# An S5 layer with a SwiGLU feed-forward: the last quarter's two sets of lag products move from behind the scan to ahead of its end

## The chip, the cores and the metric

One core of a Trainium2 chip runs the whole program. Its engines each follow their own queue of instructions: PE (matrix products), DVE, ACT and POOL (elementwise work), and SP, which here only issues transfers. The metric is the device time of one execution in microseconds (us); the time before is the median of three executions.

## The reference, cut to what matters

One layer of a diffusion backbone on 1024 latent tokens and 256 context tokens of width 1024, in fp32. With a depth of one, the only mixer is the bidirectional S5 one, followed by a SwiGLU feed-forward and a final norm; only the latent tokens are returned.

```python
def s5_direction(u_ctx, u_lat, lam_re, lam_im, log_step, b_re, b_im, c_re, c_im):
    lam_bar = jnp.exp(lam * jnp.exp(log_step)[:, None])
    b_bar = ((lam_bar - 1.0) / lam)[..., None] * lax.complex(b_re, b_im)
    def run(u, h0):
        bu = jnp.einsum('lgh,gnh->lgn', u, b_bar)
        bu = bu.at[0].add(lam_bar * h0)
        _, h = lax.associative_scan(_linear_combine, (a, bu), axis=0)
        return jnp.einsum('lgn,ghn->lgh', h, c_mat).real, h[-1]
    y_c, h_c = run(u_ctx, 0)      # the context's last state starts the latent scan
    y_l, _ = run(u_lat, h_c)
    return y_c, y_l

# both directions are added, then
y = y + d_skip * h
g = gelu(y)
mixed = g * sigmoid(g @ w_glu + b_glu)
# residual with adaLN gate, RMSNorm, (silu(h @ w1) * (h @ w3)) @ w2, residual, final RMSNorm
```

There are 64 groups of 16 channels, each with 64 complex states in each direction.

## The kernel before, in words

**The mixer.** Eight tokens form a chunk, so there are 32 context and 128 latent chunks. For every chunk and group PE makes one state input, DVE runs the recurrence over chunk ends (`scan`, L839), and the output of a chunk is the sum of two things: what its own eight tokens give each other, a product of the chunk's input with a Toeplitz matrix of 15 lags, and what the state at the chunk's start gives. The 64 groups are worked on as four quarters of 16 groups (q = 0 to 3), or as eight blocks of 8 groups (k = 0 to 7, two to a quarter).

**What sets the order.** Each engine runs its instructions in the order in which the program writes them. For this stage that order is spelled out by two strings of steps, `PROG1` and `PROG2` (L32, L33), which `run` (L954) reads from left to right. DVE's scan is written before `PROG1`; the other engines run through `PROG1` while DVE scans. Between the two strings the PSUM pools of the first stage are closed and a pool of eight banks (`pe8`, tiles named `pe`) is opened in their place. A letter is a kind of step, the number its quarter, block or half:

- C: one of four products that make a quarter's output matrices, two multiplications and an addition on POOL, or the addition elsewhere. C30 to C33 are those of the last quarter.
- K: a set of lag products (`k_mats`, L802), two sets to a quarter, so K6 and K7 are the last quarter's. A set is 72 small matrix instructions on PE into two PSUM banks, which take turns; the banks must hold zeros where no product lands. Then ACT copies each bank (L821) and issues a transfer of each copy to DRAM (L822).
- T: a transfer on SP that reads the lags back as Toeplitz matrices (`toeplitz`, L830). T12 to T15 are the last quarter's.
- P, Y: for blocks 0 to 5, the chunk's own part and the state part of the first half of the latent chunks on PE, and the copies out of PSUM on ACT.
- R, Z, z: copies of the backward direction's states in turned order, on ACT or DVE. Z and z need the end of the scan.
- N, D, H: for blocks 0 to 5, the state part of the second half on PE, its addition on DVE, and the GELU on ACT. Q: both parts of blocks 6 and 7 on PE, after T12 to T15.
- I, J: the transposed output for the gated linear unit, on PE, ACT and DVE. w, l, W: its weights' loads on SP and their split in two fp32r parts on DVE and POOL. g: its first products on PE. b, x, V: the bias, the gate and the split of further weights.
- M, m, F: modulation columns and a row, and the last states between scan steps, on POOL.

Blocks K0 to K5 lie in `PROG1`: one bank is always `kt`, zeroed once, the other one a zeroed `pw` bank for quarters 0 and 1, and `pm` for quarter 2. K6 and K7 are in `PROG2`, each with two banks of the new pool; the steps k6 and k7 take the banks, and DVE sets them to zero (L966) ahead of its own work there.

Of the kernel before, what the change touches and what calls it, by code (L numbers as in the profile page):

```python
# [25 lines left out]
HC = 16  # L26
# [2 lines left out]
MAGIC = 12582912.0  # L29
HOWS = "PPPP PPEE PEEE EEEE"  # L30
ZEN = "VVSVSVSV"
PROG1 = ("A22 B0 A26 C02 G1 A30 A34 C03 A40 K0 A44 A48 C10 K1 L2 A54 G2 C11 A60 F10 C12 F11 C13 T0 T1 T2 T3 A64 M0 M1 K2 R0 P0 Y0 Y1 K3 L3 R1 C20 P1 Y2 Y3 T4 T5 G3 T6 T7 C21 C22 C23 K4 R2 P2 Y4 Y5 K5 R3 P3 Y6 Y7 T8 T9 T10 T11 C30 C31 R4 P4 Y8 Y9 C32 C33 R5 P5 Y10 Y11 M2 m0 F30 F31")  # L32
PROG2 = ("k6 Z0 N0 Z1 Z2 D0 Z3 N1 k7 D1 Z4 H0 H1 K6 N2 D2 H2 K7 T12 T13 T14 T15 N3 Z5 D3 H3 N4 D4 z6 z7 I0 J0 I1 J1 w0 w1 l1 H4 N5 D5 I2 J2 H5 I3 J3 W0 W1 x0 x1 x2 x3"  # L33
         " Q6 H6 I4 J4 Q7 b0 I5 J5 H7 g03 g13 I6 J6 g23 g05 g15 I7 J7 V1 w20 w21 g26 x10 x11 x12 x13")
LOG2E = 1.4426950408889634
LN2H = 0.693359375
# [6 lines left out]
def s5_ffn_kernel(tc, a, out):  # L43
    nc = tc.nc
    V, S, E, PE, SY = nc.vector, nc.scalar, nc.gpsimd, nc.tensor, nc.sync
    ctx = ExitStack()
    with ctx:
        ctx.enter_context(tc.manual_schedule())
        sb = ctx.enter_context(tc.tile_pool(name="sb", bufs=1))
        def region(tag, kb, dt=F32):  # L50
            return sb.tile([P, int(kb * 256)], dt, tag=tag, name=tag)
# [12 lines left out]
        R0 = region("r0", 7)  # L64
# [79 lines left out]
        def pw(shape=(4, P)):  # L144
            return pW.tile([P] + list(shape), F32, tag="w", name="pw", bufs=NW[0])
# [613 lines left out]
        pm = pW.tile([P, 512], F32, tag="m", name="pm")  # L759
# [10 lines left out]
        def zeros(t):  # L770
            S.copy(t, cpk[:, 0:1].to_broadcast([P, 15 * HC]))
            return t

        kt = zeros(pA.tile([P, 15 * HC], F32, tag="r3", name="kt"))
# [24 lines left out]
        def bb(q, d, ri, a_):  # L799
            return BBn[q // 2][:, ri, d, 8 * (q % 2) + a_]  # L800

        def k_mats(q, hq, kts):  # L802

            tiles = [(g_, 2 * gi + hq, kts[g_][32 * gi:32 * gi + HC], slice(64 * g_, 64 * g_ + 64), (64 * g_, 32 * gi))
                     for gi in range(4) for g_ in range(2)]
            for d, c0, c1, ts_ in ((1, 128, 240, slice(7, 0, -1)), (0, 0, 112, slice(6, None, -1))):
                for ri in range(2):
                    for g_, a_, kv, ps, tp in tiles:
                        PE.matmul(kv[:, c0:c1], bb(q, d, ri, a_)[ps], CL[q][ps, ri, d, a_, ts_], start=ri == 0, stop=ri == 1,
                                  tile_position=tp)  # L810
            for g_, a_, kv, ps, tp in tiles:
                l0 = 64 * g_ + HC * (tp[1] // 32)
                PE.matmul(kv[:, 112:128], ident[ps, l0:l0 + HC], KD[ps, q, hq], start=True, stop=False, tile_position=tp)
            for d in range(2):
                for ri in range(2):
                    for g_, a_, kv, ps, tp in tiles:
                        PE.matmul(kv[:, 112:128], bb(q, d, ri, a_)[ps], Cs[q % 2][ps, 0, ri, d, a_], start=False,
                                  stop=d + ri == 2, tile_position=tp)
            for g_ in range(2):
                gq, kx = 2 * hq + g_, KX[2 * hq + g_]  # L820
                S.copy(kx, kts[g_])  # L821
                S.dma_start(KD_[q][:, gq], kx)  # L822
# [131 lines left out]
        def run(prog):  # L954


            for w in prog.split():
                op, i = w[0], int(w[1:])
                if op == "A":
                    ada(i)  # L960
                elif op == "M":
                    mod_cols(i)
                elif op == "k":
                    KT[i] = [pe8([15 * HC]) for _ in range(2)]
                    for kv in KT[i]:
                        V.memset(kv, 0.0)  # L966
                elif op == "K":
                    k_mats(*divmod(i, 2), KT.get(i) or [kt, zeros(pw([15 * HC])) if i < 4 else pm[:, 0:15 * HC]])
                elif op == "L":
                    cs_load(i, S)  # L970
                elif op == "G":
                    cs_sign(i)
                elif op == "B":
                    bb_put(1, bb_turn(1))
                    bb_put(0, bb_turn(0))
                elif op == "C":
                    q, part = divmod(i, 10)
                    for f in cl_ops(q, part, cts[q][part], HOW[q][part]):
                        f()
                elif op == "F":  # L980
                    fill(*divmod(i, 10), *((RW, 0) if i >= 30 else (RC[3], 12)))
                elif op == "T":
                    toeplitz(i)
                elif op == "R":
                    turned(i, 0, HSe[i], S)
                elif op == "Z":
                    turned(i, 1, HSl[i], ENG[ZEN[i]])
                elif op == "z":
                    turned(i, 2, HSq[i], ENG[ZEN[i]])
                elif op == "P":  # L990
                    inner[i] = x_mm(i, pw)
                    states_mm(i, inner[i], 0, HSe[i], False)
                elif op == "Q":
                    inner[i] = x_mm(i, pe8)
                    states_all(i, inner[i], HSq[i])
                elif op == "Y":
                    S.copy(yview(i // 2, i % 2), inner[i // 2][i % 2])
                elif op == "N":
                    late[i] = [pe8([4, T, HC]) for _ in range(2)]
                    states_mm(i, late[i], 1, HSl[i], True)  # L1000
                elif op == "D":
                    for gp, po in enumerate(late[i]):
                        tt(yview(i, gp), po, yview(i, gp), ADD)
                elif op == "H":
                    if i in late:
                        S.activation(Y[:, i], Y[:, i], AF.Gelu_apprx_tanh)
                    else:
                        for gp in range(2):
                            S.activation(yview(i, gp), inner[i][gp], AF.Gelu_apprx_tanh)
                elif op == "I":  # L1010
                    if GH[0] is None:
                        GH[0] = tuple(view(region(t, 16, R32), 0, [4, 8, P]) for t in ("c1", "c0"))
                    late[i] = gt_hi(i, 0)
                elif op == "J":
                    gt_lo(i, 0, late[i])
                elif op == "W":
                    if not WR:
                        W0.append(region("c2", 16, R32))
                        WR.append((view(W0[0], 0, [8 * 256]), view(W0[0], 8, [8 * 256])))
                    v = slice(1024 * i, 1024 * i + 1024)  # L1020
                    split(wr0[i], (WR[0][0][:, v], WR[0][1][:, v]), E, V)
                elif op == "w":
                    cq, h = divmod(i, 10)
                    SY.dma_start(wr0[h], a["w_glu"][cq][:, 1024 * h:1024 * h + 1024])
                elif op == "b":
                    SY.dma_start(bglu, a["b_glu"].to_broadcast([P, D]))
                elif op == "l":
                    load_glu(i)
                elif op == "m":
                    mod_row(0)  # L1030
                elif op == "x":
                    gate(i % 10, slice(4 * (i // 10), 4 * (i // 10) + 4))
                elif op == "V":
                    GR.append(region("ra", 80.5, R32))
                    GH[1] = (view(GR[0], 0, [4, 8, P]), view(GR[0], 16, [4, 8, P]))
                    WR.extend((view(GR[0], kb, [8 * 256]), view(GR[0], kb + 8, [8 * 256])) for kb in (32, 48, 64))
                    split(wraw, WR[i], E)
                elif op == "g":
                    glu_mm(0, i // 10, range(i % 10 + 1))

        KT = {}
        late, W0, WR, PZ, GH, GR = {}, [], [], {}, [None, None], []
        wr0 = [view(RXa, 4, [1024]), view(RW, 0, [1024])]
        bglu = view(RU, 32, [D])
# [5 lines left out]
        def pe8(shape, tag="e", bufs=8):  # L1050
            return pE.tile([P] + list(shape), F32, tag=tag, name="pe", bufs=bufs)
# [51 lines left out]

        HOW = [[{"P": PE, "Y": SY, "E": E, "V": V}[c] for c in h] for h in HOWS.split()]
        run(PROG1)
        psW.__exit__(None, None, None)
        psA.__exit__(None, None, None)
        psE = tc.tile_pool(name="psE", bufs=1, space=bass.MemoryType.PSUM, reuse_waits="tile")
        pE = psE.__enter__()
        run(PROG2)  # L1110
        W0, GR = W0[0], GR[0]
# [93 lines left out]
        for cq in range(4):  # L1205
            for s in range(4):
                k = 4 * cq + s
# [61 lines left out]
        G2 = region("c3", 16, R32)  # L1269
# [420 lines left out]
        for i, (kind, ft, j) in enumerate(seq):  # L1690
# [12 lines left out]
            if kind == "U":  # L1703
# [4 lines left out]
                if (ft, j) in LAST:  # L1708
                    k, h = LAST[ft, j]
# [63 lines left out]
```

## Time and profile before

| | |
|---|---|
| median of 3 executions | 1024.48 us (1022.91 to 1024.67) |
| the profiled execution's own time | 1024.33 us |
| its span, first to last instruction | 1022.5 us |
| PE busy | 962.6 us (94%) |
| DVE, ACT, POOL busy | 785.6, 438.5, 762.7 us |
| mean granted clock of PE | 0.987 of full speed |

A row of the timeline gives the start of a run of like instructions, how long it lasts, the engine, the line of the kernel, the operation, the tile written and the tiles read, and in brackets how long the engine was idle before it and what ended that wait. PEld is the weight load that belongs to a matmul and overlaps with the one before. "Granted clock" is the share of full speed that the chip let PE run at. For fp32 the trace holds two records for each matrix instruction of the program.

### The profile page before, as it was taken

The numbers are of one execution on the slowest core, as the hardware profiler recorded it, in microseconds if no ns is written. First come the engines' busy times: TensorE is split into PE (matmuls) and PEld (weight loads), VectorE is DVE, ScalarE is ACT, GpSimd is POOL, SyncE is SP. The second block draws the span as 40 slices with busy tenths as digits, with TensorE's granted clock in tenths as the row PEclk, the third lists the DMA queues.
The fourth block names the chain that finished last, engine by engine and source line by source line (L and its number), as shares of the span: only waits on it lengthen the run. The fifth ranks groups of instructions, "written<-read, shape, count | busy, mean of one in ns | idle before, by whom it ended". The sixth has DMA issues, their size and how long they took to land. (4 is left out here: it accounts for less than half of the span.)

```text
span 1022.5 us, 18552 instructions
## 1 busy us (share of the span) xinstructions
PE 962.6 (94%) x6988; PEld 774.2 (76%) x6988; DVE 785.6 (77%) x1642; ACT 438.5 (43%) x858; POOL 762.7 (75%) x590
## 2 busy tenths in 40 slices
PE   5987798868999999999999999999999999999996
PEld 1466523658999988778888888888888888888885
DVE  7989799994365778788968768585958778686977
ACT  5477622324353663533334343424333343324337
POOL 5799999991591457879686877778686877777664
PEclk9999999998999999999999999999999999999998
DMA  9765997222622021011212011121212111121205
GB/s 318 292 132 96 276 350 243 91 73 57 235 80 86 2 104 62 21 42 42 83 41 73 32 52 61 43 73 52 73 42 81 41 40 56 45 70 52 72 21 165
DMA packets 48546, 98.96 MB, mean 97 GB/s; under 512 B 4284, under 2 KB 18876, under 8 KB 47176
## 3 DMA queue, kind: packets, MB, share of 16 engines
q1 hardware_dynamic: 43272, 86.64, 25.3%
q0 software_dynamic: 2016, 7.34, 3.8%
q10 hardware_dynamic: 3168, 3.79, 1.1%
q8 instruction: 55, 0.90, 0.4%
q14 instruction: 35, 0.29, 0.1%
HBM read 84.25 MB, written 6.17 MB: 88 GB/s over the span
## 5 line engine op out<-in xcount | busy, mean ns | idle before, releaser
L77 POOL TENSOR_TENSOR c<-rxc,c 128x512 fp32r<-128x512 f32 x128 | 166.6, 1316 | 53.5 <-ACT c L1227 52.7
L1287 PE MATMUL ut<-ra,c 128*128 128x512 f32 x400 | 155.7, 389 | 1.2 <-DVE ra L77 1.2
L1286 PE MATMUL ut<-ra,c 128*128 128x512 f32 x400 | 155.7, 389 | 0.2 <-ACT ra L1227 0.2
L1288 PE MATMUL ut<-ra,c 128*128 128x512 f32 x400 | 155.6, 389 | 0.0
L1227 ACT CAST c<-rxc 128x512 fp32r<-128x512 f32 x128 | 79.1, 622 | 146.8 <-PE xt L1581 53.3
L1581 PE MATMUL xt<-c,c 128*128 128x512 f32 x540 | 129.7, 389 | 0.0
L1581 PEld LDWEIGHTS xt<-c,c 128*128 128x128 f32 x540 | 101.4, 188 | 21.0
L77 DVE TENSOR_TENSOR ru<-ru,xt 128x1024 f32<-128x1024 f32 x90 | 106.8, 1213 | 8.6 <-PE xt L1581 6.6
L77 DVE TENSOR_TENSOR ru<-ut,ru 128x512 f32<-128x512 f32 x98 | 67.1, 686 | 43.1 <-PE ut L1288 37.7
L1287 PEld LDWEIGHTS ut<-ra,c 128*128 128x128 f32 x400 | 75.1, 188 | 17.1 <-POOL rxc L77 1.5
L1286 PEld LDWEIGHTS ut<-ra,c 128*128 128x128 f32 x400 | 75.1, 188 | 16.1 <-ACT ra L1227 0.6
L1288 PEld LDWEIGHTS ut<-ra,c 128*128 128x128 f32 x400 | 75.1, 188 | 15.5
L77 POOL TENSOR_TENSOR c<-rw,c 128x512 fp32r<-128x512 f32 (+1 forms) x29 | 42.5, 1465 | 38.8 <-ACT c L1227 38.2
L1286 PE MATMUL ut<-c,c 128*128 128x512 f32 x160 | 62.3, 389 | 0.8 <-DVE rxa L77 0.8
L77 POOL TENSOR_TENSOR c<-ru,c 128x512 fp32r<-128x512 f32 (+1 forms) x39 | 55.5, 1422 | 10.1 <-ACT c L1227 5.7
L77 POOL TENSOR_TENSOR rxc<-rxc 128x512 f32<-128x512 f32 x40 | 61.5, 1536 | 1.6
L1288 PE MATMUL ut<-c,c 128*128 128x512 f32 x160 | 62.3, 389 | 0.0
L1287 PE MATMUL ut<-c,c 128*128 128x512 f32 x160 | 62.3, 389 | 0.0
L1581 PE MATMUL ut<-c,c 128*128 128x512 f32 x216 | 51.9, 389 | 0.0
L584 PE MATMUL pv<-ru,c 128*64 128x160 f32 x512 | 43.7, 312 | 7.3 <-POOL ru L77 2.6
L77 DVE TENSOR_TENSOR pe<-pe,ru 128x256 f32<-128x256 f32 x64 | 27.4, 428 | 29.5 <-ACT pe L1127 17.4
L77 DVE TENSOR_TENSOR ru<-ru,ut 128x512 f32<-128x512 f32 x76 | 47.2, 678 | 0.7 <-ACT ru L1635 0.5
(449 smaller groups left out, 2576.0 us busy)
## 6 DMA issues: line engine op xcount, KB each, us to landing
c<-in_ada_w SPq DMA_DIRECT2D x46, 256.0 KB
rxc<-in_w SPq DMA_DIRECT2D x38, 256.0 KB
rxc<-in_w SPq DMA_DIRECT2D x19, 512.0 KB
ru<-in_w SPq DMA_DIRECT2D x11, 512.0 KB
rw<-in_w SPq DMA_DIRECT2D x11, 512.0 KB
ra<-in_ada_w SPq DMA_DIRECT2D x10, 512.0 KB
ra<-in_ada_w SPq DMA_DIRECT2D x18, 256.0 KB
ru<-in_xT SPq DMA_DIRECT2D x4, 1024.0 KB
```

The source lines that it names most:

```text
L77: eng.tensor_tensor(out=o, in0=x, in1=y, op=op)
L584: PE.matmul(pv[64 * (i % 2):64 * (i % 2) + 64, ri, c0:c0 + 160], w[:, i, 64 * ri:64 * ri + 64], U[:, 8 * b + 4 * j + i], start=True, stop= ...
L1227: S.copy(o[0], x)
L1286: PE.matmul(pu, wh, bh, start=start, stop=False)
L1287: PE.matmul(pu, wh, bl, start=False, stop=False)
L1288: PE.matmul(pu, wl, bh, start=False, stop=stop)
L1581: PE.matmul(pd, w[:, cs_], b, start=j in (1, 2, 4) and n == 0, stop=n == 2, skip_group_check=j not in (1, 2, 4))
```

## The change

K6 and K7 move out of `PROG2`, to a place in `PROG1` behind Y11 (the copies of block 5) and ahead of M2, m0, F30 and F31. They use the two banks of the third quarter's sets, `kt` and `pm`, for both sets. The steps k6 and k7 and their four memsets go. T12 to T15 stay where they were in `PROG2`.

```diff
-PROG1 = ("A22 B0 ... C32 C33 R5 P5 Y10 Y11 M2 m0 F30 F31")
-PROG2 = ("k6 Z0 N0 Z1 Z2 D0 Z3 N1 k7 D1 Z4 H0 H1 K6 N2 D2 H2 K7 T12 T13 T14 T15 N3 Z5 D3 H3 N4 D4 z6 z7 I0 J0 I1 J1 w0 w1 l1 ...
+PROG1 = ("A22 B0 ... C32 C33 R5 P5 Y10 Y11 K6 K7 M2 m0 F30 F31")
+PROG2 = ("Z0 N0 Z1 Z2 D0 Z3 N1 D1 Z4 H0 H1 N2 D2 H2 T12 T13 T14 T15 N3 Z5 D3 H3 N4 D4 z6 z7 I0 J0 I1 J1 w0 w1 l1 ...
...
-                elif op == "k":
-                    KT[i] = [pe8([15 * HC]) for _ in range(2)]
-                    for kv in KT[i]:
-                        V.memset(kv, 0.0)
                 elif op == "K":
-                    k_mats(*divmod(i, 2), KT.get(i) or [kt, zeros(pw([15 * HC])) if i < 4 else pm[:, 0:15 * HC]])
+                    k_mats(*divmod(i, 2), [kt, zeros(pw([15 * HC])) if i < 4 else pm[:, 0:15 * HC]])
...
-        KT = {}
```

On PE the program before reads as follows from P5 (lines 945 and 922 into `pw`) on. The tiles `pe` are banks of the new pool, lines 809, 813 and 817 are a K set, and line 922 into `pe` is an N step: 64 rows are N0 and N1, then 32 each.

```order
L945 MATMUL pw<-ra,ru 128x128 x8
L922 MATMUL pw<-c_65,ra 64x128 x32
L922 MATMUL pe<-c_63,ra 64x128 x64
L809 MATMUL pe<-c_66,rxa 16x112 x32
L813 MATMUL pe<-r_60 16x16 x8
L817 MATMUL pe<-rxc,rxa 16x16 x32
L922 MATMUL pe<-c_64,ra 64x128 x32
```

K6 stands behind N0 and N1, and N2 follows it; K7 stands in the same way between N2 and N3. In the changed program, at the place where K6 ends and K7 begins, with the waits of each row:

```order
L817 MATMUL kt<-rxc,rxa 16x16
L817 MATMUL pm<-rxc,rxa 16x16
L809 MATMUL kt<-c_66,rxa 16x112 [waits Activation_49]
L809 MATMUL pm<-c_66,rxa 16x112 [waits Activation_49]
L809 MATMUL kt<-c_66,rxa 16x112
```

The two sets now follow each other directly, ahead of N0, and K7's first instruction on each of the two banks waits for ACT, which copies that bank for K6. Behind K7 the N steps stand in a row:

```order
L922 MATMUL pe<-c_63,ra 64x128 [waits DVE_49,Activation_49]
L922 MATMUL pe<-c_63,ra 64x128
L922 MATMUL pe<-c_63,ra 64x128 [waits DVE_49]
L922 MATMUL pe<-c_63,ra 64x128 x31
```

N0's first instruction waits for DVE and for ACT, and its third for DVE's turned copy. On ACT the copies and transfers move as follows (`ru<-pw` ahead of the piece is the copy of P5; line 902 are Z2 and Z4, and the table load belongs to the first GELU):

```order
+L821 COPY r_60<-kt 128x240
+L822 DMA kd_1249<-r_60 128x240
+L821 COPY r_60<-pm 128x240
+L822 DMA kd_1249<-r_60 128x240
+L821 COPY rw<-kt 128x240
+L822 DMA kd_1249<-rw 128x240
+L821 COPY rw<-pm 128x240
+L822 DMA kd_1249<-rw 128x240
 L902 COPY ra<-ra 128x512 x2
-L1006 ACT_TABLE_LOAD
```

Before, these four copies and four transfers stood between the GELUs of blocks 0 to 3; now they stand ahead of Z2, Z4 and the table load. SP's transfers keep their order.

More of the change, by code (lines that the diff above doesn't have):

```diff
@@ L31 @@
 ZEN = "VVSVSVSV"
-PROG1 = ("A22 B0 A26 C02 G1 A30 A34 C03 A40 K0 A44 A48 C10 K1 L2 A54 G2 C11 A60 F10 C12 F11 C13 T0 T1 T2 T3 A64 M0 M1 K2 R0 P0 Y0 Y1 K3 L3 R1 C20 P1 Y2 Y3 T4 T5 G3 T6 T7 C21 C22 C23 K4 R2 P2 Y4 Y5 K5 R3 P3 Y6 Y7 T8 T9 T10 T11 C30 C31 R4 P4 Y8 Y9 C32 C33 R5 P5 Y10 Y11 M2 m0 F30 F31")
-PROG2 = ("k6 Z0 N0 Z1 Z2 D0 Z3 N1 k7 D1 Z4 H0 H1 K6 N2 D2 H2 K7 T12 T13 T14 T15 N3 Z5 D3 H3 N4 D4 z6 z7 I0 J0 I1 J1 w0 w1 l1 H4 N5 D5 I2 J2 H5 I3 J3 W0 W1 x0 x1 x2 x3"
+PROG1 = ("A22 B0 A26 C02 G1 A30 A34 C03 A40 K0 A44 A48 C10 K1 L2 A54 G2 C11 A60 F10 C12 F11 C13 T0 T1 T2 T3 A64 M0 M1 K2 R0 P0 Y0 Y1 K3 L3 R1 C20 P1 Y2 Y3 T4 T5 G3 T6 T7 C21 C22 C23 K4 R2 P2 Y4 Y5 K5 R3 P3 Y6 Y7 T8 T9 T10 T11 C30 C31 R4 P4 Y8 Y9 C32 C33 R5 P5 Y10 Y11 K6 K7 M2 m0 F30 F31")
+PROG2 = ("Z0 N0 Z1 Z2 D0 Z3 N1 D1 Z4 H0 H1 N2 D2 H2 T12 T13 T14 T15 N3 Z5 D3 H3 N4 D4 z6 z7 I0 J0 I1 J1 w0 w1 l1 H4 N5 D5 I2 J2 H5 I3 J3 W0 W1 x0 x1 x2 x3"
          " Q6 H6 I4 J4 Q7 b0 I5 J5 H7 g03 g13 I6 J6 g23 g05 g15 I7 J7 V1 w20 w21 g26 x10 x11 x12 x13")
```

## The prediction

> **What bounds the kernel now.** First the page: which engine is busy, and at what clock.
>
> ```profile
> PE 962.6 (94%) x6988; PEld 774.2 (76%) x6988; DVE 785.6 (77%) x1642; ACT 438.5 (43%) x858; POOL 762.7 (75%) x590
> PEclk9999999998999999999999999999999999999998
> ```
>
> PE is the fullest engine, but a share over the whole span hides the stages. The view of stretches, cut where the scan ends (228.62) and where the gated linear unit's products begin (267.49), shows what the change meets (columns: length, then busy us of PE, PEld, DVE, ACT, POOL, granted clock, DMA share, GB/s).
>
> ```profile
> 228.62:267.49 38.87, 35.75 (x985) 33.31 (x985) 18.00 (x28) 14.61 (x21) 10.73 (x11) 0.91 0.40 124
> 267.49:1000.45 732.96, 730.57 (x3637) 621.46 (x3635) 544.46 (x756) 301.48 (x579) 542.86 (x396) 1.00 0.17 57
> ```
>
> After 267.49 PE is idle for 732.96 - 730.57 = 2.4 us in all. What PE gains before that point therefore reaches the end, unless another chain holds that point back (a rival below). Now the same view, cut at the steps.
>
> ```profile
> 224.00:228.70 4.70, 0.01 (x1) 0.01 (x1) 4.34 (x19) 1.17 (x3) 4.54 (x8) 0.97 0.01 3
> 228.70:236.13 7.43, 7.06 (x128) 6.57 (x128) 4.06 (x9) 3.38 (x4) 6.01 (x9) 0.56 0.01 2
> 236.13:237.75 1.62, 1.62 (x147) 1.58 (x145) 1.29 (x2) 0.19 (x1) 0.00 (x0) 1.00 0.00 0
> 237.75:241.06 3.31, 2.69 (x72) 2.38 (x65) 0.09 (x1) 1.47 (x3) 0.00 (x0) 1.00 0.25 79
> 241.06:243.92 2.86, 1.73 (x145) 1.59 (x144) 1.53 (x3) 1.06 (x1) 0.00 (x0) 1.00 0.02 6
> 243.92:249.05 5.13, 4.73 (x131) 4.42 (x129) 1.41 (x3) 2.21 (x4) 0.00 (x0) 1.00 0.18 56
> ```
>
> In order: PE waits for the scan (4.7 us idle); N0 and N1 (7.43); K6 (1.62); N2 (3.31); K7 (2.86); N3 and N4 (5.13). The two sets stand where PE is the bound, and just ahead lies a hole of 4.7 us. The timeline of PE tells what the idle time inside was.
>
> ```profile
> 228.72 0.70 PE L922 MATMUL pe<-c,ra 64*64 64x128 f32 x4 [4.71 <-DVE ra L77]
> 229.77 6.44 PE L922 MATMUL pe<-c,ra 64*64 64x128 f32 x124 [0.35 <-DVE ra L904]
> 237.75 1.76 PE L922 MATMUL pe<-c,ra 64*64 64x128 f32 x46
> 240.13 1.00 PE L922 MATMUL pe<-c,ra 64*64 64x128 f32 x18 [0.62 <-issue]
> 243.58 0.41 PE L817 MATMUL pe<-rxc,rxa 64*16 64x16 f32 x34 [1.13 <-issue]
> 247.59 1.50 PE L922 MATMUL pe<-c,ra 64*64 64x128 f32 x34 [0.40 <-issue]
> 250.04 2.27 PE L922 MATMUL pe<-c,ra 64*64 64x128 f32 x64
> 254.71 1.16 PE L945 MATMUL pe<-ra,ru 128*128 128x128 f32 x8 [0.48 <-DMA ra<-kd]
> ```
>
> Three gaps wait for "issue", nothing the profile shows. The stretches between them hold the same number of matmul records:
>
> ```profile
> 240.10:243.57 3.47, 2.33 (x128) 1.00 0.14 43
> 243.57:247.55 3.98, 3.61 (x128) 1.00 0.21 66
> ```
>
> 128 records, then a wait: I read it as instructions that reach PE in blocks of 128 records (with their weight loads), a block no sooner than 3.47 to 3.98 us after the one ahead. State products take 2.27 per 64 at full clock (the 250.04 row), 4.54 a block, and don't outrun that; a K set (72 instructions, 144 records, in 1.62 us) does.
>
> **The change part by part.** *Removed from PROG2's stage on PE:* K6, 1.62, and K7 with its gap, 2.86: 4.48 us. N2, N3 and N4 then run as N5 does, 3 x 2.27 = 6.81 in place of 3.31 + 5.13 = 8.44: 1.63 us, of which 0.62 + 0.40 are the gaps. The 0.48 us on lag matrices goes too, since their loads move up (below). Together 4.48 + 1.63 + 0.48 = 6.59 us after N1.
>
> *Removed from DVE:* four memsets.
>
> ```profile
> 228.62 0.52 DVE L966 MEMSET pe<- 128x240 f32 x2
> 229.05 0.66 DVE L904 COPY ra<-ra 128x512 f32<-128x512 f32 x1
> ```
>
> The first two stand ahead of N0's reversed copy, which can start 229.05 - 228.62 = 0.43 us sooner. I book nothing for it, because N0 will wait for something later.
>
> *Added in front: when K6 and K7 run.* K6 needs the quarter's last product from POOL, and P5 off PE (idle since 228.72 - 4.71 = 224.01).
>
> ```profile
> 220.12 2.37 POOL L77 TENSOR_TENSOR c<-c,rw 128x1024 f32<-128x1024 f32 x1
> 224.04 1.07 ACT L997 COPY ru<-pw 128x512 f32<-128x512 f32 x2 [3.09 <-PE pw L922]
> 205.49 0.36 ACT L821 COPY rw<-kt 128x240 f32<-128x240 f32 x1 [0.57 <-PE pm L817]
> 205.88 0.33 ACTq L822 DMA_DIRECT2D kd<-rw  x1
> 206.25 0.36 ACT L821 COPY rw<-pm 128x240 f32<-128x240 f32 x1 [0.40 <-ACT rw L821]
> 186.61 1.63 ACTq L822 DMA_DIRECT2D kd<-rw  x1
> ```
>
> POOL's product ends at 222.49, so K6 runs from 224.05 to 225.67; ACT is free of P5's copies by 225.11. K7 uses the same two banks, and its instructions alternate between them, so it waits for K6's two copies: 0.36 + issue + 0.36, by the rows 206.25 + 0.36 - 205.49 = 1.12 after 225.7: 226.85. Unhindered it would end at 228.47, in the scan's shadow. But the blocks: the gap at N2's 46th record puts the block edge before it 82 records back into K6, at its 62nd, and the one before that at N0's 62nd. K6 now stands where N0 stood, so the edges fall at K6's 62nd record (224.05 + 1.62 x 62 / 144 = 224.75), K7's 46th, N0's 30th. The block that starts at K7's 46th record comes at 224.75 + 3.47 to 3.98 = 228.2 to 228.7, the record being due at about 227.4. The other 98 records (1.10 us) end at 229.3 to 229.8; ACT copies the first bank (0.36), and N0, whose first bank is that one, starts at 229.75 to 230.25, later than before (229.77) by some 0.25. Its 30th record has its block at 231.7 to 232.7.
>
> *N0 and N1: the clock.* They ran at a granted 0.50 until about 235.24 (0.88 in the last row is 0.50 for 0.24 of it). PE by stretches, four of them some 3.4 us long (length, PE busy and records, clock):
>
> ```profile
> 207.90:211.30 3.40, 2.03 (x60) 1.00 0.25 70
> 211.30:214.72 3.42, 1.30 (x9) 1.00 0.59 148
> 215.00:218.00 3.00, 3.00 (x39) 0.50 0.31 94
> 224.96:228.37 3.41, 0.00 (x0) 1.00 0.00 0
> 228.37:231.80 3.43, 2.73 (x44) 0.51 0.00 0
> 235.00:236.00 1.00, 1.00 (x32) 0.88 0.00 0
> ```
>
> The clock fell to half after the stretch with 1.30 us busy and after the empty one, not after that with 2.03. Now 224.96 to 228.37 holds K6's last 0.7, K7's first 0.5 and what follows 228.2: some 1.3 us. That is nearer 1.30 than 2.03: I take the low clock. N0 and N1 then end about 0.5 us later than before, at 236.6: 0.25 for the start and some 0.3 to 1.3 of block wait, part of it made good since the clock returns at 235.24 as before. At full clock they take 4.54 and a block wait of about 1.1 from 230.0 and end at 235.65, 0.5 us sooner.
>
> TensorE: Matmul & The Clock Gate, Part 1, of the Trainium skill says that the clock halves after a window of about 3.4 us that was idle. By that rule no window would be idle here and the full-clock sum would hold; the trace does not agree as the rule stands, since the clock also fell after 1.30 us of work in 3.42.
>
> *Instruction blocks and the skill.* Runtime: NRT & Kernel Launch, Instruction fetch mechanics, of the Trainium skill has 16 KiB blocks whose crossing is mostly hidden. By that K7 would lose nothing at its 46th record; the trace does not agree here, with three gaps of 2.15 us together.
>
> *Moved copies and transfers.* On ACT four copies and four issues (4 x 0.36 + 4 x 0.33 = 2.8 us) now stand ahead of Z2, Z4 and the GELU table; ACT reaches Z2 at about 231, N2 needs it after 235. Banks: N0 to N4 take other banks of eight, each freed by an add that is done. On SP:
>
> ```profile
> 247.96 4.39 SPq L830 DMA_DIRECT2D ra<-kd  x4
> 252.40 1.87 SPq L1024 DMA_DIRECT2D rxa<-in_w_glu  x1
> 261.39 0.69 DVE L1075 CAST c<-rxa 128x1024 fp32r<-128x1024 f32 x1 [5.48 <-DMA rxa<-in_w_glu]
> 262.22 2.37 POOL L77 TENSOR_TENSOR c<-rxa,c 128x1024 fp32r<-128x1024 f32 x1 [27.35 <-DVE c L1075]
> 267.49 0.36 PE L1097 MATMUL pe<-c,c 128*128 128x256 f32 x1
> ```
>
> T12 waited for K7's transfers; these now go by about 231, so T12 to T15 start near 233, and the gate weights queued behind them on SP some 15 us sooner. Nothing waits for either then.
>
> **Sum:** 6.59 - 0.5 = 6.1 us. The profiled execution took 1024.33 (span 1022.5 and 1.83 around it), 0.15 under the median of 1024.48: 1024.33 - 6.1 = **1018.2**. The unknown prices, from both sides: the clock, 1.0 better at full speed; block waits at K7 and N0, from none (1.2 better) to gaps that stay at N2 to N4 as well (1.02) and follow K7's 1.13.
>
> **Rivals.**
> *Full clock.* The stretch counts as busy: N1 ends at 235.65, saving 6.59 + 0.5 = 7.1, **1017.2**. For it: 2.03 us kept the clock. Against: 1.30 did not.
> *No block waits.* K7 ends at 228.47 and N0 starts at 229.0: N1 ends at 235.4 at the low clock and at 233.7 at the full one, saving 7.3 or 9.0: **1017.0** or 1015.3. Against: the three gaps.
> *The gaps only move.* The 1.02 at N2 to N4 and K7's 1.13 turn up elsewhere: saving about 4.1, **1020.2**. Against: 4.54 a block is over 3.98.
> *The gate weights cap it.* POOL's first half ended at 262.22 + 2.37 = 264.59; if it stayed there, PE's first gate product could come at most 267.49 - 264.59 = 2.9 us sooner: **1021.4**. Against: its cast waited 5.48 us for a load that moves up.
> *PE is not the bound* between scan and gate, but the adds and GELUs on DVE and ACT: nothing gained, **1024.3**. Against: 18.00 and 14.61 us busy of 38.87.
> *Slower: ACT's queue holds N0.* N0's bank comes free behind K6's two issues and K7's first copy. Issues took 0.33, but one 1.63. Each us on both costs 2; beyond (6.1 / 2) + 0.33 = 3.4 us an issue the kernel is slower, at 4.5 us by 2: **1026.5**. No row is near that.
>
> **How the numbers follow.** Forecast 0.42; full clock 0.26; no block waits 0.04; gaps move 0.09; weights cap 0.07; no gain 0.07; slower 0.05. The likeliest gives 1018.2. The range runs from 1015.5 (the best sum and a little spread) to 1021.5 (the weights' cap), leaving out some 0.15. A measurement can tell about 0.2%, 2 us: faster 0.87, same 0.08, slower 0.05.
>
> **What would show it.** PE's timeline between 224 and 229 with both sets, a gap inside K7 marked issue, N0 starting near 230 with the bank's copy on ACT as releaser; no K set between N1 and N5, and N2 to N4 in about 6.8 us; no wait for the lag matrices at Q6; the first gate product near 261. The granted clock of 228.4 to 235 decides between the two likeliest cases. It would be wrong if the first gate product came 6 us sooner and the end did not, or if N0 started after 232.

## The result and the profile after

| | before | after |
|---|---|---|
| median of 6 executions each | 1024.55 us | 1016.76 us |
| lowest and highest | 1021.74 to 1026.48 | 1014.74 to 1020.9 |
| the profiled execution, its span | 1024.33, 1022.5 | 1017.54, 1015.8 |

The ratio is 0.9938, with a 95% interval of 0.9921 to 0.9956. Two further comparisons, below, gave 0.9954 and 0.9935. By medians the changed kernel is 5 to 8 us faster (7.8, 5.0 and 5.9 us in the three comparisons), and 1016.76 stands 1.4 us below the 1018.2 that was predicted.

First the page of the kernel after: the engines' busy time, and the granted clock in forty slices.

```profile
PE 961.4 (95%) x6988; PEld 773.5 (76%) x6988; DVE 778.5 (77%) x1638; ACT 438.5 (43%) x858; POOL 763.9 (75%) x590
PEclk9999999899999999999999999999999999999999
```

PE issues as many instructions as before and is busy about as long; only DVE has lost its four memsets. What became shorter is the span. The view of stretches of the kernel after (columns as in the prediction: length, busy us of PE, PEld, DVE, ACT, POOL, granted clock, DMA share, GB/s), cut where its scan ends (229.58), where N0 begins (232.21), where N1 ends (236.78), where N4 ends (243.56) and where the gate's products begin (261.10):

```profile
229.58:261.10 31.52, 29.40 (x809) 27.90 (x794) 15.33 (x24) 13.93 (x19) 16.08 (x15) 1.00 0.52 157
261.10:993.80 732.70, 730.29 (x3636) 621.46 (x3635) 539.92 (x757) 301.74 (x580) 538.66 (x392) 1.00 0.17 57
232.21:236.78 4.57, 3.92 (x116) 3.73 (x120) 1.30 (x3) 2.78 (x4) 3.54 (x5) 1.00 0.25 68
236.78:243.56 6.78, 6.78 (x214) 6.66 (x210) 4.60 (x9) 3.92 (x4) 0.00 (x0) 1.00 0.74 170
243.56:261.10 17.54, 17.30 (x377) 16.45 (x377) 7.55 (x12) 6.87 (x11) 9.96 (x6) 1.00 0.56 191
```

From the scan's end to the gate's first product it is 31.52 us where it was 38.87: 7.35 us less. (The 228.62 at which the prediction cuts is the start of the memset behind the scan; the scan's last instruction ended at 228.57, as 229.58 is read here.) The stretch behind the gate's start is as long as it was (732.70 beside 732.96, with the same 2.4 us of idle PE), so what was gained ahead of it reached the end. The scan itself ended 1.0 us later in this execution (229.58 beside 228.57), which is why the two spans differ by 6.7 us and not by 7.4. That end moves between executions of one kernel too: it lay at 229.58, 228.82 and 228.39 in the three profiles of the changed kernel.

PE's timeline of the kernel after, from K7's first products on:

```profile
228.24 0.36 PE L809 MATMUL kt<-c,rxa 64*16 64x112 f32 x2 [0.47 <-ACT r L821]
228.99 0.27 PE L809 MATMUL pm<-c,rxa 64*16 64x112 f32 x1 [0.40 <-ACT r L821]
230.57 0.25 PE L809 MATMUL pm<-c,rxa 64*16 64x112 f32 x1 [0.76 <-issue]
232.21 1.27 PE L922 MATMUL pe<-c,ra 64*64 64x128 f32 x30 [0.47 <-ACT rw L821]
234.14 6.12 PE L922 MATMUL pe<-c,ra 64*64 64x128 f32 x190 [0.65 <-issue]
249.39 0.60 PE L945 MATMUL pe<-ra,ru 128*128 128x128 f32 x4 [0.24 <-issue]
```

K7 is stopped three times: twice until ACT has copied a bank of K6, then at a gap marked issue. N0 does not start when the scan ends but 2.63 us later, on ACT's copy of K7's first bank, and is stopped once more at its 30th record. The old gaps inside N2 to N4 are gone (6.78 us, all of it busy), and so is the wait for lag matrices at Q6; a gap of 0.24 us marked issue stands near its place. ACT, DVE, SP and POOL of the kernel after:

```profile
227.82 0.36 ACT L821 COPY r<-kt 128x240 f32<-128x240 f32 x1 [0.58 <-PE pm L817]
228.58 0.36 ACT L821 COPY r<-pm 128x240 f32<-128x240 f32 x1 [0.40 <-ACT r L821]
231.80 0.36 ACT L821 COPY rw<-kt 128x240 f32<-128x240 f32 x1 [2.86 <-PE pm L817]
229.29 0.29 DVE L77 TENSOR_TENSOR ra<-ltc,ra 128x128 f32<-128x128 f32 x1
234.69 4.17 SPq L830 DMA_DIRECT2D ra<-kd  x4
238.91 1.93 SPq L1020 DMA_DIRECT2D rxa<-in_w_glu  x1
251.14 2.72 POOL L77 TENSOR_TENSOR c<-rxa,c 128x1024 fp32r<-128x1024 f32 x1 [15.28 <-DVE c L1070]
```

N0's releaser, the copy at 231.80, had itself been waiting for PE. The scan's last instruction on DVE ends at 229.29 + 0.29 = 229.58. The Toeplitz loads start at 234.69 in place of 247.96, the gate's weights at 238.91 in place of 252.40, and POOL's split of them is done with its first half at 253.86, 7.2 us before PE asks for it.

### The profile page after: what moved, and what is told of

Its sections match the earlier page's. It is cut to its first block, busy times and chain, and to the rows that moved or that the text cites. A ratio compares the mean times of both kernels' runs of the same rounds, so it can differ in the third digit from the quotient of the medians.

```text
span 1015.8 us, 18556 instructions
## 1 busy us (share of the span) xinstructions
PE 961.4 (95%) x6988; PEld 773.5 (76%) x6988; DVE 778.5 (77%) x1638; ACT 438.5 (43%) x858; POOL 763.9 (75%) x590
## 5 line engine op out<-in xcount | busy, mean ns | idle before, releaser
L77 POOL TENSOR_TENSOR c<-rw,c 128x512 fp32r<-128x512 f32 (+1 forms) x29 | 39.8, 1371 | 37.5 <-ACT c L1222 37.5
L77 POOL TENSOR_TENSOR c<-ru,c 128x512 fp32r<-128x512 f32 (+1 forms) x39 | 58.8, 1507 | 10.1 <-ACT c L1222 5.7
```

Source lines behind the costliest of these rows:

```text
L77: eng.tensor_tensor(out=o, in0=x, in1=y, op=op)
```

## The experiments

All ratios are to the kernel before, run beside the experiment on the same chip, with 95% intervals. There were three such comparisons. The first holds the change again, the products issued a second time, the sets left out and K7's own banks; the second the products ahead, the four large products, one set and the memsets; the third the change once more, the repeats of K7's own banks and of one set, and one set with two large products. "Scan to gate" is the time from the scan's end to the gate's first product in the profiled execution; behind that product all fourteen profiles take 754.6 to 755.1 us to the end. It is 38.9 us in the kernel before and 31.5 in the one after.

The theory to be tested: the gain is PE time. Two sets of lag products stood in a stretch that PE bounds, and now run in a hole of the scan; part is given back because instructions reach PE in blocks and because N0 now waits for K7's copy. The rivals: the gain comes from the earlier loads of lag matrices and gate weights, or from the four memsets that left DVE, or from the clock.

### The change itself, twice more

No edit. The first belongs to the first comparison, the second to the third.

> The changed kernel once more, beside the three that follow and the kernel before on the same chip. Both theories: 5 to 9 us under the kernel before.

> The changed kernel, beside the other three of this set on one chip. 5 to 8 us under the kernel before.

Measured: 0.9954 (0.9936 to 0.9972) and 0.9935 (0.9916 to 0.9955); scan to gate 33.1 and 30.6 us. In the first the clock fell, in the second it did not. The stretches of the first, and the one from N0 to the gate in all three profiles (first run again, second run again, kernel after):

```profile
225.99:229.40 3.41, 2.16 (x128) 1.54 (x128) 3.11 (x14) 0.72 (x2) 3.33 (x6) 1.00 0.20 63
229.40:232.81 3.41, 2.77 (x122) 2.63 (x124) 0.84 (x1) 0.84 (x3) 3.33 (x5) 0.50 0.17 53
232.81:236.22 3.41, 3.41 (x71) 3.41 (x67) 0.88 (x2) 2.30 (x3) 2.27 (x4) 0.50 0.25 52
231.59:261.96 30.37, 29.68 (x697) 28.60 (x697) 13.40 (x22) 13.66 (x18) 13.03 (x11) 0.92 0.50 159
```
```profile
230.43:258.98 28.55, 28.11 (x697) 26.84 (x697) 13.43 (x22) 13.57 (x18) 13.76 (x12) 1.00 0.53 162
```
```profile
232.21:261.10 28.89, 28.00 (x696) 26.84 (x697) 13.45 (x22) 13.57 (x18) 13.50 (x11) 1.00 0.55 167
```

So one program has both of the prediction's likeliest cases. The low clock costs 30.37 less 28.55 or 28.89: 1.5 to 1.8 us from N0 on. It fell after a stretch of 3.41 us in which PE was busy for 2.16, and in this execution came back only after one that was busy throughout.

The first of them also shows the instruction blocks. Its timeline of PE, at K6's 62nd record and at K7's 46th, and the stretch between the two:

```profile
226.14 0.25 PE L809 MATMUL pm<-c,rxa 64*16 64x112 f32 x1 [0.29 <-issue]
229.59 0.34 PE L809 MATMUL pm<-c,rxa 64*16 64x112 f32 x1 [0.43 <-issue]
226.14:229.59 3.45, 2.16 (x128) 1.53 (x128) 3.15 (x13) 0.72 (x2) 3.37 (x6) 0.97 0.24 76
```

From one gap to the next it is 128 records and 3.45 us. In the kernel after the pair K7's 46th and N0's 30th record lies 234.14 - 230.57 = 3.57 us apart. All fourteen profiles agree: between P5 and the gate, every distance from one gap marked issue to the next is 128 records (fourteen pairs), 256 (one) or 382 to 384 (five).

### The two sets' products issued a second time in the old places

The changed kernel, with the products of K6 and K7 issued again, without copies or transfers, behind N1 and behind N2, into banks of the new pool. Everything that the change moved early stays early; only PE has the old work in the old places again.

```diff
-PROG2 = ("Z0 N0 Z1 Z2 D0 Z3 N1 D1 Z4 H0 H1 N2 D2 H2 T12 ...
+PROG2 = ("Z0 N0 Z1 Z2 D0 Z3 N1 D1 Z4 H0 H1 j6 N2 D2 H2 j7 T12 ...
-        def k_mats(q, hq, kts):
+        def k_mats(q, hq, kts, copy=True):
-            for g_ in range(2):
+            for g_ in range(2 if copy else 0):
+                elif op == "j":
+                    k_mats(*divmod(i, 2), [pe8([15 * HC]) for _ in range(2)], False)
```

> The changed kernel with the matrix products of K6 and K7 issued a second time, without copies or transfers, at their old places behind N1 and N2; the results are not used. Theory (the gain is PE time taken out of a stage that PE bounds): 4.5 us of the gain go, with the block gaps some 5.5, and the kernel lies 1 to 3 us under the kernel before. Rival (the gain comes from the lag matrices and gate weights being loaded 15 us sooner, or from ACT's and DVE's relief): these stay, so the gain of 6 to 8 us stays.

Measured: 1027.32 us, 1.0046 (1.0025 to 1.0066), 9.4 us above the change run beside it and 4.4 above the kernel before, where the theory had 1 to 3 below; scan to gate 42.1 us. The stretch from N0 to the gate, and PE's two larger gaps in it:

```profile
231.23:270.69 39.46, 34.40 (x984) 32.19 (x985) 13.53 (x22) 13.55 (x18) 13.13 (x11) 0.96 0.39 123
241.71 2.79 PE L922 MATMUL pe<-c,ra 64*64 64x128 f32 x50 [2.46 <-issue]
256.03 0.75 PE L922 MATMUL pe<-c,ra 64*64 64x128 f32 x11 [1.52 <-issue]
```

With the old work back on PE not only is the whole gain gone: the kernel is slower than before, although its loads come early and the memsets are gone. Against the full-clock run of the change above, PE is busy 6.3 us longer (34.40 - 28.11), of which at most some 1.6 us, an estimate, are the clock (0.96 over 39.46 us), and idle 4.6 us longer (5.06 against 0.44), nearly all of it marked issue. The direction is the theory's. The size is not: the two sets cost 3.2 us by their duration, and this stage lost 10.9 (39.46 - 28.55). The theory of blocks gives a reason: a set that PE could run in 1.6 us is 144 records, and so more than a block, and a block came every 3.3 to 4.0 us.

### The sets left out

The changed kernel without K6 and K7. It leaves out the last quarter's lag products, copies and transfers; T12 to T15 read the third quarter's lags in their place.

```diff
-... R5 P5 Y10 Y11 K6 K7 M2 m0 F30 F31")
+... R5 P5 Y10 Y11 M2 m0 F30 F31")
-            rows = KD_[q][32 * gi:32 * gi + HC]
+            rows = KD_[min(q, 2)][32 * gi:32 * gi + HC]
```

> The changed kernel without K6 and K7 at all, their copies and transfers included; T12 to T15 read the third quarter's lags instead, so the last quarter's output is not the reference's. Theory (the sets now lie in the scan's shadow and cost at most the wait of N0): within 1 us of the changed kernel on either side, with the granted clock back at 0.50 over N0 and N1 since the hole of 4.7 us is empty again, and N0 starting about 0.7 us behind the scan's end. Rival (the moved sets still cost PE time): 3 us or more faster than the changed kernel.

Measured: 1016.02 us, 0.9926 (0.9901 to 0.9952), beside 0.9954 (0.9936 to 0.9972) for the change: 1.9 us lower by the medians, with intervals that overlap. That lies between the theory (within 1 us) and the rival (3 us or more). Its timeline and a stretch:

```profile
227.95 0.69 PE L922 MATMUL pe<-c,ra 64*64 64x128 f32 x4 [3.56 <-DVE ra L77]
228.00:230.00 2.00, 1.56 (x20) 1.17 (x24) 1.87 (x2) 1.98 (x3) 2.00 (x4) 0.50 0.98 194
```

N0 starts the moment the scan ends (227.95, 0.05 behind it), and at half clock. So in their new place the two sets cost about 2 us by the medians, of the 4.5 that their rows had before. They may pay for a part of what they delay at N0: with them PE is at work in the hole, and in some executions the clock stays up. That part is not measured by itself.

### K7 in banks of its own

The changed kernel, with K7 in two banks of the `pw` pool that ACT sets to zero between block 5's copies, so that it need not wait for K6's copies.

```diff
-... R5 P5 Y10 Y11 K6 K7 M2 m0 F30 F31")
+... R5 P5 q7 Y10 q7 Y11 K6 K7 M2 m0 F30 F31")
-                    k_mats(*divmod(i, 2), [kt, zeros(pw([15 * HC])) if i < 4 else pm[:, 0:15 * HC]])
+                    k_mats(*divmod(i, 2), [kt, zeros(pw([15 * HC])) if i < 4 else pm[:, 0:15 * HC]] if i < 7 else KB7)
+                elif op == "q":
+                    KB7.append(zeros(pw([15 * HC])))
+        KB7 = []
```

> The changed kernel with two banks of its own for K7 (two pw banks, zeroed by ACT ahead of Y10 and between Y10 and Y11), so that K7 waits for no copy of K6 and N0 for no copy of K7. Theory (K7's end is set by the instruction block that is due at its 46th record): the waits for ACT of 0.9 us inside K7 go, the gap marked issue in K7 grows by about as much, N0 starts at most 0.5 us sooner after the scan, and the time is within 1 us of the changed kernel. Rival (the bank copies set it): no gap grows, N0 starts 1.3 us sooner and the kernel is 1.3 us faster.

> The changed kernel with two banks of its own for K7, once more. Theory (the block at K7's 46th record decides, the copies only a little): 0 to 1.5 us under the changed kernel, with the gap in K7 at some 1.7 us again. Rival: no difference.

Measured: 1016.25 us, 0.9934 (0.991 to 0.9958), and in the repeat 1017.38, 0.9945 (0.9925 to 0.9966), where the change itself had 0.9954 and 0.9935: 1.7 us below it, then 1.2 above it, no difference that these runs can tell. PE's timeline of the first:

```profile
226.34 0.92 PE L809 MATMUL pw<-c,rxa 64*16 64x112 f32 x45
228.94 0.46 PE L809 MATMUL pw<-c,rxa 64*16 64x112 f32 x18 [1.68 <-issue]
```

K7 now starts at once, with no wait for ACT, and runs 45 records. Then it waits 1.68 us for issue where the change waited 0.76 and 0.43 behind its two waits of 0.47 and 0.40. In the repeat the gap is 1.45. The waits for K6's copies were cover for the next block; taking them away gave the time to the gap. This is the most direct evidence that the 46th record of K7 has an arrival of its own, which no bank decides.

The repeat adds a case to the clock: it fell to half after a stretch with 1.79 us busy.

```profile
224.87:228.28 3.41, 1.79 (x107) 1.54 (x110) 3.11 (x13) 0.65 (x2) 3.33 (x6) 1.00 0.24 77
228.28:231.69 3.41, 3.41 (x68) 3.41 (x72) 0.69 (x1) 2.50 (x4) 3.33 (x5) 0.50 0.27 87
```

### The products ahead, with nothing else moved

The kernel before, with K6's and K7's products also issued ahead of the scan's end, without copies (steps j6 and j7, into `kt` and `pm`). PE has the new early work and all the old work; the loads stay late.

```diff
-PROG1 = "... R5 P5 Y10 Y11 M2 m0 F30 F31"
+PROG1 = "... R5 P5 Y10 Y11 j6 j7 M2 m0 F30 F31"
+                elif op == "j":
+                    k_mats(*divmod(i, 2), [kt, pm[:, 0:15 * HC]], False)
```

> The kernel before (K6 and K7, their copies, transfers and memsets at the old places), with the matrix products of K6 and K7 also issued ahead of the scan's end, without copies or transfers, their results unused. PE then has the same instructions in the same order as where the products were put back behind N1 and N2; what differs is that lag matrices and gate weights come late as before. Theory (PE's instructions decide): within 1.5 us of that kernel, so 3 to 6 us slower than the kernel before. Rival (the early loads are a part of the gain): 2 us or more slower than that kernel.

Measured: 1025.22 us, 1.0021 (1.0006 to 1.0036), 2.3 us above the kernel before, less than the 3 to 6 that were expected. This is nearly what the run with the products issued a second time does, except for where the copies, the loads and the memsets stand. With early loads that one was at 1.0046 (1.0025 to 1.0066), with late ones this is at 1.0021: no gain from early loads can be seen. What makes the other 2 us slower is open; the two belong to different comparisons. The timeline of PE in this run, and of DVE:

```profile
229.26 0.34 PE L809 MATMUL pm<-c,rxa 64*16 64x112 f32 x1 [2.10 <-issue]
231.00 0.51 DVE L966 MEMSET pe<- 128x240 f32 x2 [2.77 <-PE pm L817]
```

Without any wait for ACT the gap at K7's 46th record is 2.10 us, the largest at this place, as the theory of blocks has it: the less else holds K7, the longer it waits there. DVE's memset of the new banks waits for the end of the early products (2.77 us), and so N0 starts 2.5 us behind the scan here too.

### Only the clock: four large products in the hole

The kernel before, with four 128x512 products of no use issued into `pm` where the change puts K6 and K7. They are eight records, so the gap in N2 moves by eight records only (from its 46th to its 38th), and they keep PE busy.

```diff
-PROG1 = "... R5 P5 Y10 Y11 M2 m0 F30 F31"
+PROG1 = "... R5 P5 Y10 Y11 u4 M2 m0 F30 F31"
+                elif op == "u":
+                    for _ in range(i):
+                        PE.matmul(pm, ident, view(RU, 0, [512]), start=True, stop=True)
```

> The kernel before, with four large products (128x512, fp32, 8 records of 0.4 to 0.6 us) in the hole ahead of the scan's end and nothing else changed; their results are unused. They keep PE busy for some 3 us with few instructions. If the granted clock stays at 1.00 over N0 and N1, these take 4.6 us in place of 6.4, and the kernel is 1 to 2 us faster: what the clock alone is worth. If the clock falls to 0.50 all the same, no change within 1 us.

Measured: 1020.22 us, 0.9971 (0.996 to 0.9983); scan to gate 35.6 us. The stretch of the four products, and PE's row for N0 and N1:

```profile
226.00:229.00 3.00, 3.00 (x8) 1.14 (x6) 2.85 (x11) 1.65 (x4) 2.92 (x5) 1.00 0.00 0
229.12 4.30 PE L922 MATMUL pe<-c,ra 64*64 64x128 f32 x128
```

The clock stays at full speed, and N0 and N1 take 4.30 us where they took 7.43. Four useless products make the kernel before 3.0 us faster by the ratio (1.7 to 4.1), more than the 1 to 2 that were expected, although they run past the scan's end and N0 starts 1.13 us behind it in place of 0.15. So a full clock is worth about 3 us in that kernel. In the changed kernel, where less work meets the low clock, it is the 1.5 to 1.8 us above.

TensorE: Matmul & The Clock Gate, Part 1, of the Trainium skill tells of an idle window of about 3.4 us after which the clock halves, and of one that runs freely. Stretches of 3.41 us fit these profiles, and so does a phase that differs between executions of one program; that the window must be idle does not fit, since the clock also fell after stretches with 1.79 and 2.16 us busy.

### One set moved, alone and with two large products behind it

The kernel before, with K6 moved as in the change, and K7 left where it was with its step k7 and its two memsets. The second kernel also puts two useless 128x512 products behind K6, into a `pw` bank (a step u2 between K6 and M2, as u4 above).

```diff
-PROG1 = "... R5 P5 Y10 Y11 M2 m0 F30 F31"
-PROG2 = "k6 Z0 N0 Z1 Z2 D0 Z3 N1 k7 D1 Z4 H0 H1 K6 N2 D2 H2 K7 T12 ..."
+PROG1 = "... R5 P5 Y10 Y11 K6 M2 m0 F30 F31"
+PROG2 = "Z0 N0 Z1 Z2 D0 Z3 N1 k7 D1 Z4 H0 H1 N2 D2 H2 K7 T12 ..."
```

> The kernel before with only K6 moved ahead of the scan's end; K7 stays behind N2 with its own banks and memsets. Theory: K6's 1.62 us, N2's gap and ramp (0.6 to 1.0) and half a memset go, some 2.5 to 3.5 us faster than the kernel before, about half of the whole change. Rival (what counts is the last transfer, K7's, and the loads that wait for it): less than 1 us faster.

> Only K6 moved, once more. In the first look it was as fast as the whole change. If moving K7 as well pays what it takes off the stage (2.9 us), this kernel is 2 us or more slower than the changed one; if K7 in front puts N0 off by about as much as it saves, it is within 1.2 us of it.

> Only K6 moved, and behind it two large products (128x512, fp32, results unused) fill the rest of the hole ahead of the scan's end. Theory (the low clock over N0 and N1 is what the one set leaves on the table, and few instructions cost no block): granted clock 1.00 over N0 and N1, 1 to 2 us faster than with K6 alone, and level with or faster than the changed kernel by up to 2 us. Rival (the clock falls or its worth is lost behind the blocks): within 0.7 us of K6 alone.

Measured: with one set 1018.43 us, 0.9952 (0.9936 to 0.9968), and in the repeat 1018.96, 0.9963 (0.995 to 0.9977), where the change had 1016.18, 0.9935 (0.9916 to 0.9955). With the two large products behind it, beside that repeat, 1016.59, 0.9942 (0.9927 to 0.9958). The timelines of N0 to N2, of the one set alone (its repeat) and then with the large products, each with a stretch inside them:

```profile
228.30 8.11 PE L922 MATMUL pe<-c,ra 64*64 64x128 f32 x192 [1.56 <-DVE ra L77]
230.00:232.00 2.00, 2.00 (x44) 0.50 0.03 8
```
```profile
228.50 6.69 PE L922 MATMUL pe<-c,ra 64*64 64x128 f32 x192
230.00:232.00 2.00, 2.00 (x74) 1.00 0.03 8
```

One set moved takes most of the gain: 3.1 to 4.5 us (1022.1 - 1018.96, and 1022.88 - 1018.43), with N0 at 0.14 us behind the scan in place of 2.0 to 2.8, and the clock low. The second set is worth 2.8 us by the medians of the repeat and 1.7 by its profiled executions (1017.18 and 1015.45), where it takes 2.86 off the stage by its rows and delays N0. The two intervals overlap a little, and in the first two comparisons one set (0.9952) stood as low as the change (0.9954), so that it pays is likely and its size is open. Two useless products give the one set 2.4 us by medians, 1.2 by profiles (1015.94), and make it level with the change. So the change's second set and those two products pay about the same. By the rows one takes work from PE's stage and the other holds the clock. Neither kernel is faster than the change by these intervals.

### The memsets on ACT

The kernel before, with the four banks zeroed on ACT and not on DVE.

```diff
                     for kv in KT[i]:
-                        V.memset(kv, 0.0)
+                        zeros(kv)
```

> The kernel before with the four banks zeroed on ACT in place of DVE's four memsets. Theory: DVE's turned copy starts 0.4 us sooner, N0 with it, and the time is 0 to 0.5 us lower, not to be told from no change. Rival (the memsets ahead of N0's turned copy are a main part of the gain): 1.5 us or more faster.

Measured: 1022.28 us, 0.9994 (0.9982 to 1.0005). The memsets are no part of the gain that can be measured.

## Why the prediction was right, point by point

**What bounds the stage: right, and tested.** PE's work between scan and gate sets the end. Put back, it took all of the gain away, with the early loads still in place; the memsets gave nothing when tried apart; all profiles have 754.6 to 755.1 us behind the gate's first product. The rivals of a bound on DVE and ACT and of a cap by the gate's weights fall with that: the first gate product came at 261.10 (predicted near 261), with the weights ready at 253.86. Nor is it the clock alone: at the low clock on both sides, scan to gate is 33.1 us after the change (its first run again) and 38.9 and 37.7 with the old order (the kernel before, and the memsets on ACT), so 4.6 to 5.8 us are gained without it.

**What is removed: 6.59 predicted, 7.0 measured.** From N1's end to the gate it was 267.49 - 236.13 = 31.36 us before and is 261.10 - 236.78 = 24.32 now. N2 to N4 take 6.78 (6.81 predicted), so K6, K7 and the gaps gave 12.92 - 6.78 = 6.14 (6.11 predicted). The rest is the stage behind. The lag-matrix wait of 0.48 us went, as predicted. The 0.24 us marked issue that stands near its place is not a rest of it but a gap of the kind of the blocks: it lies 382 records behind the one at N0's 30th. And Q6's state products took 4.24 us in place of 4.79, which the prediction had not in its sum. Their rows in PE's timeline, before and after:

```profile
255.80 4.79 PE L935 MATMUL pe<-c,ra 64*64 64x128 f32 x128
```
```profile
249.93 4.24 PE L935 MATMUL pe<-c,ra 64*64 64x128 f32 x128
```

This 0.55 us is not shown to be the change's: in all thirteen other profiles these products take 4.24 to 4.27 us, in the kernels with late loads too (4.26 with the memsets on ACT, 4.25 with the products ahead). Only the one profile of the kernel before had them longer. Without it the removal is 6.5 us, beside the 6.59 predicted.

**When N0 starts: too early by 0.4 to 1.6 us against the scan.** The prediction had 229.75 to 230.25, 1.1 to 1.6 us behind the scan's end; measured were 2.63, 2.77 and 2.04 us behind it. The mechanisms were the ones named: K7 behind K6's two copies, the gap at its 46th record, N0 on the copy of K7's first bank. The arrival of blocks was sized rightly, at 3.29 to 3.84 us in the twelve pairs of gaps with 128 records between them outside the profile before, beside the 3.47 to 3.98 used. The term that failed is the hole. The 4.6 us between P5's end and the scan's end (224.01 to 228.62) were taken from one profile, and they are 3.43, 3.94 and 3.78 us in the three profiles of the changed kernel: P5 ended at 226.15 in the one above, not at 224.01. All that was laid behind P5 shifted with it, by 0.7 to 1.2 us against the scan. Over all fourteen profiles the hole runs from 2.4 to 5.5 us. One of the prediction's own signs of being wrong came with this: N0 starting after 232. It started at 232.21 in the profiled execution, 1.0 us of it by the scan's later end.

**The clock: forecast low, the profiled execution had it full.** This is the step by which the prediction's likeliest case and its first rival differed. The granted clock was 1.00 throughout N0 and N1 after the change, 0.50 in the first run of it again, and 1.00 in the second. The prediction read a threshold of busy time from two rows, between 1.30 and 2.03 us. That reading falls. In each trace the clock changes only at marks that lie a multiple of 3.41 us apart, and the marks lie elsewhere in each execution, so the stretch that the prediction laid at 224.96 to 228.37 is not one of the kernel after. In that kernel the clock was low from 216.59 to 220.00, and the third stretch of 3.41 us behind that held 2.12 us of work and was followed by the full clock; with K7's own banks it was kept after 1.90. It fell after 1.79 and 2.16 (PE alone, the kernel after twice, then K7's own banks: length, busy us and records, clock, DMA share, GB/s):

```profile
216.59:220.00 3.41, 3.25 (x32) 0.50 0.36 104
226.83:230.24 3.41, 2.12 (x150) 1.00 0.18 57
230.24:233.65 3.41, 2.44 (x128) 1.00 0.19 61
```
```profile
225.36:228.77 3.41, 1.90 (x157) 1.00 0.22 70
228.77:232.18 3.41, 2.80 (x128) 1.00 0.15 50
```

Where the low clock came it cost 1.5 to 1.8 us from N0 on, where the prediction had 1.0. Not its length was wrong: it lay over N0 and N1 for 4.6 us (231.59 to 236.22), less than the 5.2 assumed (230.0 to 235.24). What is off is the block wait with which the prediction charged the full clock: 1.1 us at N0's 30th record, where 0.65 and 0.38 were measured. At the low clock no gap shows there, and one of 0.69 us comes two blocks later, at N4's 30th record:

```profile
243.36 1.49 PE L922 MATMUL pe<-c,ra 64*64 64x128 f32 x34 [0.69 <-issue]
```

**N1's end: right by luck, by two errors that cancel.** Predicted 236.6, measured 236.78. N0 came 2.0 to 2.5 us later than the start predicted, 1.0 of it with the scan, and at full clock N0 and N1 took 4.57 us with their block wait, 1.8 to 2.3 less than the prediction had for them at the low clock. A sum that lands does not show that its terms were right.

**The time.** On the two profiled executions the gain is 1024.33 - 1017.54 = 6.8 us for 6.1 predicted: 7.0 behind N1, less 0.65 that N1 ended later, 0.3 behind the gate and 0.1 outside the span. By medians it is 7.8, 5.0 and 5.9 in the three comparisons, on both sides of 6.1. The full-clock rival had 1017.2, the forecast 1018.2. The profiled execution was the rival's case, the first run of the change again the forecast's; which of the two a median stands for is not shown, since only the profiled executions have a clock for this stage. The range's lower end of 1015.5 was set a little above the prediction's own best sum, 1015.3.

**The other rivals.** That K7 and N0 see no block waits is refuted by 0.43 to 0.76 us at the 46th record, and by 1.45 to 2.10 where ACT's waits are taken away. That the gaps only move came partly true: 0.76 + 0.65 us at K7 and N0 and 0.24 at Q6 stand where 1.02 + 1.13 stood. (By its own terms this rival saves 6.1 - 2.15 = 3.95 us, not the 4.1 that the prediction gives.) The issues of K6's and K7's transfers on ACT took 0.33 us, one 0.57, far from the 3.4 at which ACT's queue would have made the change a loss.

Runtime: NRT & Kernel Launch, Instruction fetch mechanics, of the Trainium skill holds the crossing of a 16 KiB block mostly hidden. If these gaps are such crossings, which their distance of 128 records suggests and no run proves, it is not hidden in this stage, with 1.65 us of it after the change and about 5 us with the sets issued twice.

**What stays open.** What decides the clock in a hole that is partly filled with small products. Busy time alone does not (1.90 us kept it and 2.16 did not); large products kept it up in both kernels that had them, and no run tells whether it is the work of the products, their size, or the phase of the stretch that counts.

## What to carry to other kernels

Where an engine that bounds a stage stands idle just ahead of it, work moved into the idle time takes its whole duration off the stage, and more where it also divides a stream that comes in blocks. From that goes what it delays the stage's first instruction: here N0 started 2.0 to 2.8 us behind the scan, in place of 0.15. Cost this delay from the spread of the hole over several executions, not from one profile. Count instructions as well as microseconds: a set of small products that runs in 1.6 us but is longer than a block of instructions costs PE a block's arrival, and a wait taken away ahead of that edge only becomes a wait at it. A few large products in a hole can hold the clock, and are worth trying on their own before work is moved for that purpose.

## What the runs showed of the hardware

PE's unexplained gaps lay 128 matrix records apart, or a multiple of that to within two records, in every one of twenty distances, and neighbouring ones came 3.29 to 4.00 us after each other; in the stage with the sets issued twice that was worth more (4.6 us of idle time) than the time of the products put back (3.2). Four 128x512 products without use made a kernel of 1022.88 us 3.0 us faster (1.7 to 4.1). And the same program met the low clock in one profiled execution and the full clock in two, after stretches of one length with like busy time (2.16 beside 2.12 and more), which moves its time by 1.5 to 1.8 us and is about as large as what the second set of products brings.
